# Gate stores, key reads and token-sum loads of an attention stage put in another order on the DMA queues

## The chip, the cores and the metric

The kernel runs on one core of one Trainium2 chip. The core's engines are TensorE (PE, with its weight loads shown apart as PEld), VectorE (DVE), ScalarE (ACT), GpSimd (POOL) and SyncE (SP), which only issues DMAs here; ACT issues some DMAs too. The metric is the device time of one execution in microseconds, the median of several runs. All matrix products run in float32 split in a high and a low part, so that one logical product is three passes (high by high, high by low, low by high).

## The reference

The input is 1024 tokens of width 1024, with 16 learned meta tokens put ahead (1040 rows). One block is computed:

```python
h = rms_norm(x)
q_a, k_a, v_a, q_b, k_b, v_b, gate_a, gate_b = split(h @ w_in)
y_a = differential_attention(q_a, k_a, v_a)    # 4 heads, two softmaxes each, full 1024 x 1040
y_b = windowed_gqa(q_b, k_b, v_b, sink)        # 8 heads, 128-token windows
m = sigmoid(gate_a) * (y_a @ w_ba) + sigmoid(gate_b) * (y_b @ w_bb)
h = x + m @ w_o
h = h + (silu(rms_norm(h) @ w_g) * (rms_norm(h) @ w_u)) @ w_d
out = rms_norm(h)[16:]
```

What matters for this change: the two gates are one product of all 1024 tokens with 2048 columns of `w_in`, and in differential attention each head has two score maps m = 0, 1 with the softmax of the one subtracted from that of the other.

## The kernel before

The stages follow each other: input norm and the projections of q, k and v with the windowed attention in between (to about 294 us of the span), then differential attention with the gate products as filler between its steps (294 to 626 us), then the branch products, the output product, and the feed-forward block (626 us to the end), which is nearly all matmuls.

*Projections.* `project_kva(h)` makes the keys of head h: `k_consume` (L656) stores each chunk of keys, high and low part, into a DRAM buffer `ka_d[h][m]` of 128 rows, 64 of the high part and 64 of the low part (L658). One DMA per map m and chunk; three chunks of 384, 384 and 272 columns.

*Loading a head.* `load_a(h)` (L922 on) issues, first for m = 1 and then for m = 0, the queries `aq` (L929) and the keys `ak` on SP. The keys are wanted twice on chip: as variant 0 with the high part in partitions 0 to 63 and the low part below (one DMA of 520 KB, L930), and as variant 1 with the two swapped (two DMAs of 260 KB, L932). `load_v(h)` (L938) brings the values `av` (L940 to L942). All loads of a head have one buffer each, so a head's loads wait for the last use by the head before.

*Scores.* `scores_a(h, t)` (L966) multiplies a tile of 128 queries with the keys, in three column chunks per map; the first chunk of the first map (m = 1, variant 0) is the first thing that needs `aq` and `ak`. DVE adds the distance bias (L969, L973), ACT takes the exponential (L977), DVE combines both maps (L983), `transpose_a` (L995 on PE, L998 on ACT, L999 on DVE) turns the tile and `values_a` (L1008) multiplies with `av`.

*Gates.* `gate_steps` (L868) computes the gate product with a Strassen-like scheme of seven products per column block k: in its first part the products named 1, 2 and 6 for all eight k (n = 0 to 23, in the order `first_g`), in the second the products 5, 7, 3, 4 of each k (n = 24 to 55). I write (k, p) for product p of block k; the order begins (0,1), (1,1), (0,2), (1,2), (2,1), (3,1), (2,2), (3,2), (4,1), (4,2). A product is 12 matmuls of 128x512, given out in four steps of three by `fill`. Two PSUM banks are shared by all. The products need sums of token halves and of weights: the weight operand `wopg` is made by POOL (L799 a cast, L800 a subtraction) from raw weights `wg` that SP loads (L760); the token sums were stored in DRAM as `t_d` earlier and are loaded over parts of the activations `hT_hi` and `hT_lo` by `turn_into(i)` (L820, two DMAs of 1 MB, for i = 1 eight of 256 KB), as soon as the products that use the old contents are out: i = 2 behind head 0's values, i = 0 after (7,1), i = 3 after (7,2), i = 1 after (4,6). i = 0 is first read by (0,5), i = 1 by (0,7), i = 3 by (0,4).

*Results of the gate products* leave PSUM by an ACT copy (L874, L881) or a DVE addition (L885, L899) into small tiles: tag `u` with 4 buffers for the parts kept, tag `g` with 3 buffers for finished ones. They are stored in `u_d` and `g_d`. For the first five blocks (k < 5) products 1 and 2 are stored by DMAs that ACT itself issues:

```python
nc.scalar.copy(p1, ps)
if k < 5:
    nc.scalar.dma_start(u_d[k], p1)
```

*Order.* A scheduler that simulates the engines orders the instructions on each engine, except inside `tc.manual_schedule(engines=...)`, where the program's own order holds for the engines named. One such stretch for PE and POOL opens ahead of the loop over the 32 (head, tile) pairs; at n = 5 (`BY_HAND`) it is closed, and one for PE alone is opened. For head 0 the loop starts with 24 steps of gate products (`G_FIRST`, six products), and only then come scores, five gate steps to a tile. `tc.issue_after(i)` only asks that an instruction stands behind i in its queue. The DMAs of the built program signal on eight semaphores used in rotation, whichever engine issues them; a DMA waits in its issuing engine's queue until the DMA eight before it has landed.

Of the kernel before, what the change touches and what calls it, by code (L numbers as in the profile page):

```python
# [19 lines left out]
P = 128  # L20
# [3 lines left out]
L = S + NM  # L24
# [24 lines left out]
WB_BUFS = 3  # L49
G_HEAD = 6  # L50
G_FIRST = 24
BY_HAND = 5

QK_BUFS = 3
W_BUFS = 2
# [20 lines left out]
def encoder_block(ctx: ExitStack, tc: tile.TileContext, x, meta, norm_mix, w_in, lq1, lk1, lq2, lk2,  # L76
# [7 lines left out]
    def f32(ap):  # L84
        return ap.bitcast(F32)
# [14 lines left out]
        return p.tile([P, 512], F32, tag=tag, name=name, bufs=bufs)  # L100

    qa_d = [dram.tile([2, P, S], F32, name=f"qa_d{h}") for h in range(AH)]
    ka_d = [dram.tile([2, P, L], F32, name=f"ka_d{h}") for h in range(AH)]
    va_d = [dram.tile([P, 2, 9, P], F32, name=f"va_d{h}") for h in range(AH)]
    g_d = [dram.tile([P, S], F32, name=f"g_d{i}") for i in range(16)]
    t_d = [dram.tile([P, 2, 4, 512], F32, name=f"t_d{i}") for i in range(4)]
# [548 lines left out]
    def project_kva(h):  # L655
        def k_consume(st, at, n):  # L656
            for m in range(2):
                nc.sync.dma_start(ka_d[h][m, :, at:at + n].rearrange("(a d) t -> d a t", a=2),  # L658
                                  st[64 * m:64 * m + 64, :, :n])

        def va_evac(pt, k0, nb, kp):
            vs = stage.tile([P, 2, 4, P], F32R, tag="qk", name="va_stage", bufs=QK_BUFS)
            hi, lo = vs[:kp, 0, :nb, :], vs[:kp, 1, :nb, :]
            nc.scalar.activation(hi, pt, AF.Copy)
            nc.vector.tensor_tensor(lo, pt, f32(hi), ALU.subtract)
            nc.sync.dma_start(va_d[h][:kp, :, k0:k0 + nb, :], f32(vs)[:kp, :, :nb, :])

        project_v(C_VA + h * P, f"va{h}", va_evac)
        project(C_KA + h * P, K_CHUNKS, f"ka{h}", evac_split(None, k_consume))
# [89 lines left out]
                    after.enter_context(tc.issue_after(keys_a[0].ins))  # L759
                raws_g.append(nc.sync.dma_start(w, w_in[:, col:col + P].rearrange("(c p) n -> p c n", p=P)))  # L760

    sums_g, keys_a, raws_g, values_in = {}, [], [], []

    def weights_g(n):
        k, p = order_g[n]
# [39 lines left out]
            n_made[0] += 1  # L805

    RIGHT_G = {1: (0, 0), 6: (0, 1), 2: (1, 0), 5: (0, 0), 7: (0, 1), 3: (1, 1), 4: (1, 0)}
    LAST_T = {(7, 1): (0,), (7, 2): (3,), (4, 6): (1,)}
    INTO_T = {2: (0, 1), 0: (0, 0), 1: (0, 1), 3: (1, 0)}

    def turn_into(i):

        d, t = INTO_T[i]
        for c in (range(4) if i == 1 else (slice(0, 4),)):
            for hl, h in enumerate((hT_hi, hT_lo)):
                with ExitStack() as after:
                    if i == 2:
                        after.enter_context(tc.issue_after(values_in[0].ins))
                    to = f32(h)[:, 4 * d:4 * d + 4, HALF[t]]
                    nc.sync.dma_start(to[:, c], t_d[i][:, hl, c])  # L820

    def gate_steps():
        banks, kept = {}, {}

        def stage_g(name):
            return gstage.tile([P, 512], F32, tag="g", name=name, bufs=G_BUFS)

        def kept_g(name):
            return gstage.tile([P, 512], F32, tag="u", name=name, bufs=4)

        def store(src, o, t, queue=nc.sync):
            queue.dma_start(g_d[o][:, HALF[t]], src)

        held_pp, last_pp = [None, None], [-1, -2]

        def take(n, k, p):
            i = min((i for i in range(2) if held_pp[i] is None), key=last_pp.__getitem__)
            held_pp[i], last_pp[i] = (k, p), n
            return bank(psum2, f"pp{i}", f"pg_{k}_{p}", 1)

        add = nc.vector.tensor_tensor
        for n, (k, p) in enumerate(order_g):
            ensure_g(n + 1)
            k_next = {(5, 1): 0, (6, 1): 1, (7, 1): 2, (7, 6): 3, (2, 6): 4, (3, 6): 0}.get((k, p), k + 1 if p == 7 and k < 7 else None)
# [12 lines left out]
            if p in (1, 2):  # L857
                banks[1, k] = banks.get((1, k), banks[1])
            ps = banks[1, k] if p in (1, 2) else banks[{3: 5, 4: 7}.get(p, p)]
            for i in range(2):  # L860
                if held_pp[i] == (k, {2: 1, 3: 5, 4: 7}.get(p, p)):
                    last_pp[i] = n
                    if p not in (1, 5, 7):
                        held_pp[i] = None
            d, t = RIGHT_G[p]
            for c in range(4):
                for i, (x, h) in enumerate(((0, hT_hi), (0, hT_lo), (1, hT_hi))):
                    nc.tensor.matmul(ps, op[:, x, c, :], h[:, 4 * d + c, HALF[t]],  # L868
                                     start=(p in (1, 6, 7) and c == 0 and i == 0),
                                     stop=(p in (2, 6, 3, 4) and c == 3 and i == 2), skip_group_check=True)  # L870
                if c == 3:
                    if p == 1:
                        p1 = kept_g(f"p1_{k}")
                        nc.scalar.copy(p1, ps)  # L874
                        if k < 5:
                            nc.scalar.dma_start(u_d[k], p1)
                        else:
                            kept[k] = p1
                    elif p == 2:
                        st = stage_g(f"g11_{k}")  # L880
                        nc.scalar.copy(st, ps)  # L881
                        store(st, 2 * k, 0, nc.scalar if k < 5 else nc.sync)
                    elif p == 6:
                        u = kept.pop(k)
                        add(u, ps, u, ALU.add)  # L885
                        nc.sync.dma_start(u_d[k], u)
                    elif p == 5:
                        kept["q"] = kept_g(f"q_{k}")
                        nc.scalar.copy(kept["q"], ps)
                    elif p == 7:  # L890
                        st = stage_g(f"g22_{k}")
                        add(st, ps, kept.pop("q"), ALU.add)
                        store(st, 2 * k + 1, 1)
                    else:
                        st = stage_g(f"g{p}_{k}")
                        if p == 3:
                            nc.scalar.copy(st, ps)
                        else:
                            add(st, ps, kept[k], ALU.add)  # L899
                        store(st, 2 * k + (p == 4), int(p == 3))  # L900
                    for i in LAST_T.get((k, p), ()):
                        turn_into(i)
                    if p == 4:
                        del kept[k]
                yield
            ensure_g(n + 4)
# [15 lines left out]
    def load_a(h):  # L922
        p = apool
        qs, ks = [None, None], [None, None]
        for m in (1, 0):
            q = qs[m] = p.tile([P, S], F32R, tag=f"q{m}", name=f"aq{h}_{m}")
            k = ks[m] = p.tile([P, 2, L], F32R, tag=f"k{m}", name=f"ak{h}_{m}")
            with tc.issue_after(raws_g[3].ins):
                nc.sync.dma_start(f32(q), qa_d[h][m])  # L929
            nc.sync.dma_start(f32(k)[:, 0, :], ka_d[h][m])  # L930
            for hl in range(2):
                last = nc.sync.dma_start(f32(k)[64 - 64 * hl:128 - 64 * hl, 1, :], ka_d[h][m, 64 * hl:64 * hl + 64, :])  # L932
        keys_a.append(last)
        v = p.tile([P, 2, 9, P], F32R, tag="v", name=f"av{h}")
        nc.gpsimd.memset(f32(v)[:, 0, 8, :], 0.0)
        return qs, ks, v

    def load_v(h, va):  # L938
        with tc.issue_after(keys_a[h].ins if h else raws_g[4].ins):
            nc.sync.dma_start(f32(va)[:, :, 0:8, :], va_d[h][:, :, 0:8, :])  # L940
            nc.sync.dma_start(f32(va)[:2 * NM, 0, 8, :], va_d[h][:2 * NM, 0, 8, :])
            values_in.append(nc.sync.dma_start(f32(va)[2 * NM:3 * NM, 0, 8, :], va_d[h][:NM, 1, 8, :]))  # L942
        if not h:
            turn_into(2)

    sum_a = {}

# [122 lines left out]

    for n in range(AH * NT + T_LAG):
        scoring, turning = iter(()), iter(())
        if n == BY_HAND:
            order_pe.__exit__(None, None, None)
            order_pe = tc.manual_schedule(engines={mybir.EngineType.PE})
            order_pe.__enter__()
        if n == 1:
            fill(2)
        if n < AH * NT:
            h, t = divmod(n, NT)  # L1080
            if t == 0:
                if not h:
                    ensure_g(2)
                ld = load_a(h)
                if h:
                    load_v(h, ld[2])
                fill(G_HEAD if h else G_FIRST)
                if not h:
                    load_v(h, ld[2])
            if t % 2 == 0:  # L1090
                at_ = apool.tile([P, 9, 2, 256], F32R, tag="at", name=f"at{h}_{t}", bufs=AT_BUFS)
            s = [None, None]
# [767 lines left out]
```

## Time and profile before

| | us |
|---|---|
| median of 3 runs | 1436.69 (1436.20 to 1436.83) |
| the profiled execution | 1435.76 |
| its span, first to last instruction | 1433.9 |
| TensorE busy in the span | 1404.5 (98%) |
| TensorE idle from 290 to 640 us | 19.0, of it one pause of 9.0 and one of 2.6 |

Times in the profile are microseconds from the start of the span. A timeline row gives start and duration, engine, line and operation, and, in brackets, how long the engine had stood idle and what ended that. ACTq and SPq are the issues of DMAs on those engines' queues; the time to landing counts from the issue. In a table of windows, each row is a stretch of the span with the busy time of each engine (and its instructions), the clock that TensorE was granted as a share of full speed, the DMA engines' busy share and the data rate.

### The profile page before, as it was taken

Reading aid. Unit: us, or ns where it says so; the run is one execution under the profiler, and the core shown is the slowest. Engines: PE = TensorE matmul, PEld = TensorE weight load, DVE = VectorE, ACT = ScalarE, POOL = GpSimd, SP = SyncE. Lnnn points to the kernel's source line nnn. Section 1 sums busy time; section 2 is a strip of 40 time slices with the busy share of each in tenths; the row PEclk is TensorE's granted clock in tenths of the full one; section 3 lists DMA queues with packets and bytes.
Section 4 is the critical chain, followed back from the end, with each engine's and each line's share of the span. In section 5 each row is a group of like instructions: output and inputs, shape, how many; then the busy total and the mean of one; then the engine's idle time right before and its main releaser. Section 6 shows DMA issues by size and latency. Waiting matters only on the chain.

```text
span 1433.9 us, 20696 instructions
## 1 busy us (share of the span) xinstructions
PE 1404.5 (98%) x7183; PEld 1205.7 (84%) x7183; DVE 911.6 (64%) x1584; ACT 672.5 (47%) x1284; POOL 634.6 (44%) x648
## 2 busy tenths in 40 slices
PE   9999999979999999999999999999999999999997
PEld 8998999968888888888888888888888888888886
DVE  6555666507778777755978966645544543787566
ACT  6355555414445554555346654333333333444454
POOL 4156865435677767232603044454544442000442
PEclk9999999989999999999999999999999999999999
DMA  8445564386696554197341624423332232954343
GB/s 235 95 127 161 147 199 141 101 273 195 200 327 208 166 163 148 38 317 235 116 154 75 206 88 144 150 97 109 106 107 96 96 109 99 359 183 144 121 130 141
DMA packets 193274, 226.15 MB, mean 158 GB/s; under 512 B 17336, under 2 KB 126336, under 8 KB 193168
## 3 DMA queue, kind: packets, MB, share of 16 engines
q1 hardware_dynamic: 189808, 219.36, 47.7%
q10 hardware_dynamic: 3360, 5.45, 1.2%
q8 instruction: 57, 0.93, 0.3%
q14 instruction: 49, 0.40, 0.1%
HBM read 152.48 MB, written 65.73 MB: 152 GB/s over the span
## 4 chain that ended last, share of the span: by engine, by line
PE 90%; DVE 4%; DMA 3%; ACT 1%; issue 1%; SPq 1%; POOL 0%; ACTq 0%; DVEq 0%; POOLq 0%
PE pg L1623 29%; PE pd L1727 14%; PE pg L868 7%; PE ppa L724 6%; PE po L1526 4%; PE aps L966 3%; PE pp_va L231 3%; PE pp_qb L231 3%; PE pp_qa L231 3%; PE pp_ka L231 3%; PE apy L1008 3%; DMA ak<-ka_d 2%; PE bps L398 2%; PE po L1534 2%; PE apt L995 1%; PE bpy L438 1%
## 5 line engine op out<-in xcount | busy, mean ns | idle before, releaser
L1623 PE MATMUL pg<-t,wop 128*128 128x512 f32 x1056 | 242.4, 389 | 0.0
L1623 PEld LDWEIGHTS pg<-t,wop 128*128 128x128 f32 x1056 | 198.3, 188 | 41.1
L121 POOL TENSOR_TENSOR wop<-wf,wop 128x512 fp32r<-128x512 f32 x114 | 150.7, 1323 | 164.1 <-ACT wop L120 152.7
L1727 PE MATMUL pd<-ob,oa 128*128 128x512 f32 x924 | 209.9, 389 | 0.0
L1727 PEld LDWEIGHTS pd<-ob,oa 128*128 128x128 f32 x924 | 173.3, 188 | 36.4 <-DVE ob L121 0.4
L1623 PE MATMUL pg<-b,wop 128*128 128x512 f32 x792 | 183.3, 389 | 0.0
L868 PE MATMUL pg<-hT_hi,wopg 128*128 128x512 f32 x448 | 171.9, 405 | 9.8 <-ACT g L881 9.0
L1623 PEld LDWEIGHTS pg<-b,wop 128*128 128x128 f32 x792 | 148.5, 188 | 30.7
L120 ACT ACTIVATE wop<-wf 128x512 fp32r<-128x512 f32 x128 | 80.7, 632 | 72.5 <-PE pg L1623 51.6
L121 POOL TENSOR_TENSOR oa<-ra,oa 128x512 fp32r<-128x512 f32 x27 | 34.9, 1294 | 168.9 <-ACT oa L120 167.5
L868 PEld LDWEIGHTS pg<-hT_hi,wopg 128*128 128x128 f32 x448 | 85.7, 191 | 22.6 <-issue 9.4
L977 ACT ACTIVATE as<-as,amn 128x1040 f32<-128x1040 f32 x64 | 74.5, 1165 | 59.0 <-DVE amn L973 59.0
L120 ACT ACTIVATE oa<-ra 128x512 fp32r<-128x512 f32 x77 | 48.7, 632 | 108.2 <-PE pd L1727 50.7
L966 PE MATMUL aps<-ak,aq 128*128 128x352 f32 (+1 forms) x384 | 87.7, 336 | 4.7 <-DMA ak<-ka_d 2.6
L969 DVE CUSTOM_DVE_ANT_0 as<-aps,dist,far_a 128x704 f32<-128x704 f32 x64 | 60.3, 942 | 48.9 <-POOL wopg L799 28.0
L868 PE MATMUL pg<-hT_lo,wopg 128*128 128x512 f32 x224 | 89.3, 399 | 0.0
L1400 DVE TENSOR_TENSOR s<-wf,wf 128x512 f32<-128x512 f32 x22 | 15.2, 693 | 110.7 <-DMA wf<-in_w_ff_up_dram 70.5
L966 PEld LDWEIGHTS aps<-ak,aq 128*128 128x128 f32 x384 | 65.1, 191 | 15.1 <-DVE amn L969 4.4
L400 DVE CUSTOM_DVE_ANT_0 bs<-bps,tbx,nsink 128x432 f32<-128x432 f32 (+1 forms) x64 | 38.5, 627 | 56.4 <-PE bps L398 34.9
L998 ACT ACTIVATE at<-apt 128x512 fp32r<-128x512 f32 (+1 forms) x96 | 45.3, 484 | 55.0 <-PE apt L995 55.0
L410 POOL TENSOR_SCALAR bs<-bs,bdn 128x432 f32<-128x432 f32 (+1 forms) x64 | 36.9, 596 | 76.7 <-DVE bdn L408 48.9
L1008 PEld LDWEIGHTS apy<-at,av 128*128 128x128 f32 x400 | 54.2, 190 | 4.1
(321 smaller groups left out, 3128.9 us busy)
## 6 DMA issues: line engine op xcount, KB each, us to landing
ra<-aop SPq DMA_DIRECT2D x77, 256.0 KB, 2.6
wf<-in_w_ff_gate_dram SPq DMA_DIRECT2D x25, 512.0 KB, 3.5
wf<-in_w_ff_up_dram SPq DMA_DIRECT2D x25, 512.0 KB, 3.6
aop<-as SPq DMA_DIRECT2D x44, 256.0 KB, 2.1
w_c<-in_w_in_dram SPq DMA_DIRECT2D x17, 512.0 KB, 4.9
aop<-c SPq DMA_DIRECT2D x33, 256.0 KB, 2.0
t_d<-tst SPq DMA_DIRECT2D x16, 512.0 KB, 4.1
wg_s<-in_w_in_dram SPq DMA_DIRECT2D x16, 512.0 KB, 6.2
```

The source lines that it names most:

```text
L120: high = nc.scalar.activation(hi, src, AF.Copy)
L121: lo_eng.tensor_tensor(lo, src, f32(hi), ALU.subtract)
L231: product = nc.tensor.matmul(ps[:, :n], a[:, c, :], b[:, c, at:at + n], start=(u == 0), stop=(u == 3 * DC - 1))
L724: nc.tensor.matmul(ps, w[:, a, j, :], src(j, b, tk), start=(j == 0 and n == 0), stop=(j == 3 and n == 2))
L868: nc.tensor.matmul(ps, op[:, x, c, :], h[:, 4 * d + c, HALF[t]], start=(p in (1, 6, 7) and c == 0 and i == 0), stop=(p in (2, 6, 3, 4) and ...
L966: nc.tensor.matmul(ps[:, :n], qs[m][:, t * P:(t + 1) * P], ks[m][:, vv, k0:k0 + n], start=(vv == 0), stop=(vv == 1))
L969: nc.vector.tensor_tensor_reduce(s[m][:, 0:2 * n].rearrange("p (a k) -> p a k", a=2), two[:, :, :n], dist[:, u0:u0 + 2 * n].rearrange("p ( ...
L977: nc.scalar.activation(s[m][:, 0:L], s[m][:, 0:L], AF.Exp, bias=mn[:, m, 1:2], scale=-1.0, accum_out=dn[:, 1:2] if m else first_sum)
L1008: nc.tensor.matmul(py[:, cols], v[:kp, a, k, :], at_[:kp, k, b, :], start=(k == 0 and j == 0), stop=(k == 8))
L1526: nc.tensor.matmul(sets_o[p][u], oa[:, a, u * P:(u + 1) * P], ob[:, b, :], start=(p in (1, 5) and j == 0 and k == 0), stop=(p in (2, 3) an ...
L1623: nc.tensor.matmul(ps, op[:, x, c, :], b[:, y, c, :], start=(p in (1, 5) and c == 0 and n == 0), stop=(p in (4, 2, 3) and c == 3 and n == ...
L1727: nc.tensor.matmul(ps[u], oa[:, a, u * P:(u + 1) * P], ob[:, b, :], start=(p in (1, 2, 5) and j == 0 and k == 0), stop=(p in (2, 3, 4) and ...
```

## The change

It has five parts.

1. Key storage: `ka_d` has 192 rows, and the high part of the keys is stored a second time in rows 128 to 191 (one more DMA per map and chunk: 24 in all).
2. Key reads: variant 1 is read by one DMA of 128 partitions from rows 64 to 191 instead of two of 64. A head's keys come in four DMAs, before in six.
3. Stores of gate results no longer go through ACT. `store` and the stores of `u_d` put them in a list, and `flush_stores` issues that list on SP, behind head 0's values.
4. Token sums: `turn_into(2)` comes after head 0's 24 gate steps, `turn_into(0)` after (7,6) and behind head 1's values, `turn_into(3)` together with `turn_into(1)` at (4,6) and behind `turn_into(0)`.
5. Order: for head 0 four weight operands are made ahead of the values' load, the values are loaded ahead of the 24 steps, and the stretch ordered by hand on PE and POOL ends right after those 24 steps (before, at n = 5), with a stretch for PE alone opened there.

```diff
-BY_HAND = 5
...
-    ka_d = [dram.tile([2, P, L], F32, name=f"ka_d{h}") for h in range(AH)]
+    ka_d = [dram.tile([2, 192, L], F32, name=f"ka_d{h}") for h in range(AH)]
...
             for m in range(2):
-                nc.sync.dma_start(ka_d[h][m, :, at:at + n].rearrange("(a d) t -> d a t", a=2),
+                nc.sync.dma_start(ka_d[h][m, 0:P, at:at + n].rearrange("(a d) t -> d a t", a=2),
                                   st[64 * m:64 * m + 64, :, :n])
+                nc.sync.dma_start(ka_d[h][m, P:192, at:at + n], st[64 * m:64 * m + 64, 0, :n])
...
-    LAST_T = {(7, 1): (0,), (7, 2): (3,), (4, 6): (1,)}
+    LAST_T = {(7, 6): (0,), (4, 6): (1, 3)}
...
                     if i == 2:
-                        after.enter_context(tc.issue_after(values_in[0].ins))
+                        after.enter_context(tc.issue_after(raws_g[5].ins))
+                    elif i == 0:
+                        after.enter_context(tc.issue_after(values_in[1].ins))
+                    elif i == 3:
+                        after.enter_context(tc.issue_after(turned_t[0].ins))
...
-        def store(src, o, t, queue=nc.sync):
-            queue.dma_start(g_d[o][:, HALF[t]], src)
+        held_stores = []
+
+        def store(src, o, t):
+            held_stores.append((g_d[o][:, HALF[t]], src))
+
+        def flush_stores():
+            if values_in:
+                with tc.issue_after(values_in[0].ins):
+                    while held_stores:
+                        nc.sync.dma_start(*held_stores.pop(0))
...
                         if k < 5:
-                            nc.scalar.dma_start(u_d[k], p1)
+                            held_stores.append((u_d[k], p1))
...
-                        store(st, 2 * k, 0, nc.scalar if k < 5 else nc.sync)
+                        store(st, 2 * k, 0)
...
-                        nc.sync.dma_start(u_d[k], u)
+                        held_stores.append((u_d[k], u))
...
+                    flush_stores()
...
-            nc.sync.dma_start(f32(k)[:, 0, :], ka_d[h][m])
-            for hl in range(2):
-                last = nc.sync.dma_start(f32(k)[64 - 64 * hl:128 - 64 * hl, 1, :], ka_d[h][m, 64 * hl:64 * hl + 64, :])
+            for v in range(2):
+                last = nc.sync.dma_start(f32(k)[:, v, :], ka_d[h][m, 64 * v:64 * v + P, :])
...
-        if not h:
-            turn_into(2)
...
-        if n == BY_HAND:
-            order_pe.__exit__(None, None, None)
-            order_pe = tc.manual_schedule(engines={mybir.EngineType.PE})
-            order_pe.__enter__()
...
                 ld = load_a(h)
-                if h:
-                    load_v(h, ld[2])
+                if not h:
+                    ensure_g(4)
+                load_v(h, ld[2])
                 fill(G_HEAD if h else G_FIRST)
                 if not h:
-                    load_v(h, ld[2])
+                    turn_into(2)
+                    order_pe.__exit__(None, None, None)
+                    order_pe = tc.manual_schedule(engines={mybir.EngineType.PE})
+                    order_pe.__enter__()
```

More of the change, by code (lines that the diff above doesn't have):

```diff
@@ L760, in load_g @@
                 raws_g.append(nc.sync.dma_start(w, w_in[:, col:col + P].rearrange("(c p) n -> p c n", p=P)))
-    sums_g, keys_a, raws_g, values_in = {}, [], [], []
+    sums_g, keys_a, raws_g, values_in, turned_t = {}, [], [], [], {}
     def weights_g(n):
@@ L817, in turn_into @@
                     if i == 2:
-                        after.enter_context(tc.issue_after(values_in[0].ins))
+                        after.enter_context(tc.issue_after(raws_g[5].ins))
[3 more added lines that the diff above has]
+                        after.enter_context(tc.issue_after(turned_t[0].ins))
                     to = f32(h)[:, 4 * d:4 * d + 4, HALF[t]]
-                    nc.sync.dma_start(to[:, c], t_d[i][:, hl, c])
+                    last = nc.sync.dma_start(to[:, c], t_d[i][:, hl, c])
+        turned_t[i] = last
     def gate_steps():
```

## The prediction

> **What bounds the kernel now.** I read the page first, then PE's waits, then the chain and the timelines around the waits found. The page says that PE bounds:
>
> ```profile
> span 1433.9 us, 20696 instructions
> ```
> ```profile
> PE 1404.5 (98%) x7183; PEld 1205.7 (84%) x7183; DVE 911.6 (64%) x1584; ACT 672.5 (47%) x1284; POOL 634.6 (44%) x648
> ```
>
> 29.4 us are idle, and the change removes no matmul, so it can gain only idle time and time at a lowered clock. PE's waits from 300 to 640 us (line, releaser, us in total, times, longest) show two single pauses:
>
> ```profile
> PE pg L868 <- ACT g L881: 9.0, 1, 9.0
> PE aps L966 <- DMA ak<-ka_d: 2.6, 1, 2.6
> ```
>
> The windows around both (stretch, PE, PEld, DVE, ACT, POOL busy, granted clock, DMA share, GB/s):
>
> ```profile
> 24.00:290.00 266.00, 266.00 (x1616) 245.78 (x1615) 157.40 (x380) 141.00 (x330) 146.26 (x155) 1.00 0.49 138
> 307.50:316.60 9.10, 0.09 (x2) 0.08 (x1) 0.00 (x0) 0.58 (x1) 2.96 (x4) 0.73 1.06 288
> 316.60:321.80 5.20, 5.20 (x12) 4.06 (x13) 0.00 (x0) 0.58 (x1) 1.89 (x2) 0.50 1.04 408
> 394.90:397.50 2.60, 0.00 (x1) 0.04 (x1) 0.00 (x0) 0.47 (x1) 2.40 (x2) 0.90 1.03 318
> 397.50:400.40 2.90, 2.90 (x9) 2.61 (x10) 1.56 (x3) 0.00 (x0) 1.92 (x3) 0.50 0.60 172
> ```
>
> After each pause PE has half its clock for a while. A gate matmul at full clock takes 0.227 us, from the first and the 60th of them in PE's timeline, (307.16 - 293.76)/59:
>
> ```profile
> 293.76 0.39 PE L868 MATMUL pg<-hT_hi,wopg 128*128 128x512 f32 x1
> ```
> ```profile
> 307.16 0.39 PE L868 MATMUL pg<-hT_hi,wopg 128*128 128x512 f32 x1
> 316.56 0.77 PE L868 MATMUL pg<-hT_hi,wopg 128*128 128x512 f32 x1 [9.01 <-ACT g L881]
> ```
>
> So 12 matmuls in 5.2 us lose 5.2 - 2.7 = 2.5, and 2.9 us at 0.50 lose 1.45. The first pause costs 9.0 + 2.5 = 11.5, the second 2.6 + 1.45 = 4.05. [...]
>
> ACT's timeline shows where the 9.0 come from:
>
> ```profile
> 302.14 0.59 ACT L881 COPY g<-pg 128x512 f32<-128x512 f32 x1 [2.13 <-PE pg L868]
> 315.38 0.33 ACTq L832 DMA_DIRECT2D g_d<-g  x1
> 315.82 0.58 ACT L881 COPY g<-pg 128x512 f32<-128x512 f32 x1 [13.09 <-DMA ak<-ka_d]
> ```
>
> The store of the copy made at 302.14 shares its semaphore with head 0's last key load and stands in ACT's queue until that landed, and the next copy, for which PE's bank waits, stands behind it. In the chain (start, us, what) those loads are:
>
> ```profile
> 298.70 2.07 SPq L929
> 300.87 6.90 DMA ak<-ka_d
> 307.78 7.52 DMA ak<-ka_d
> 316.56 5.46 PE pg L868 x12
> ```
> ```profile
> 388.53 8.83 DMA ak<-ka_d
> 397.50 1.22 PE aps L966 x3
> ```
>
> **The change, part by part.** *Stores off ACT: the first pause, -11.5.* Ten stores leave ACT's queue, so (3,1) no longer waits at 307.4.
>
> *What is late next on PE.* The hand-ordered stretch ends after the 24 gate steps, and in the changed kernel as built the scheduler has put head 0's first score matmul (variant 0 of m = 1) ahead of them: behind the second matmul of (1,2). That is 38 matmuls after 293.76, at this row:
>
> ```profile
> 302.40 0.61 PE L868 MATMUL pg<-hT_hi,wopg 128*128 128x512 f32 x2
> ```
>
> PE is in order there and stops until queries and keys have landed. Before, the first keys landed at 307.77 (chain: 300.87 + 6.90). Their time shifts twice. The keys' second store adds issues to an SP queue that is packed just ahead of the loads:
>
> ```profile
> 296.05 1.25 SPq L658 DMA_DIRECT2D ka_d<-qk_stage  x2
> 297.40 1.25 SPq L760 DMA_DIRECT2D wg_f<-in_w_in_dram  x2
> ```
>
> 0.62 us each; of those added I count three that find no idle time: +1.9. The other way, the two 256 KB stores that ACT issued here now come after the keys:
>
> ```profile
> 297.38 0.40 ACTq L876 DMA_DIRECT2D u_d<-p  x1
> ```
> ```profile
> 300.10 0.33 ACTq L876 DMA_DIRECT2D u_d<-p  x1
> ```
>
> From 307.78 to 315.30, 2.08 MB landed, 0.28 MB/us, so each is worth 0.9; the first had nearly landed before the keys started, so I count one and a half: -1.3. Landing at 308.4, bounds 305.9 (only the gain) and 309.7 (only the loss). PE stands 6.0 us (3.5 to 7.3), and between 1.45 and 2.5 for the half clock afterwards, I take 2.0: together 8.0 (5.0 to 9.8). The first pause thus shrinks by 3.5 (1.7 to 6.5).
>
> *The wait that takes its place on ACT.* Tag `g` has three buffers, so the fourth copy, of (3,2), needs the first store landed. That store now stands on SP behind head 0's values and both loads of token sums i = 2. In the rows of DMA issues (KB each, us to landing) the second of them, issued at 314.18, takes:
>
> ```profile
> hT_lo<-t_d SPq DMA_DIRECT2D x1, 1024.0 KB, 15.8
> ```
>
> It landed at 330.0, while ACT's queue moved four stores beside it that now come later, from that at 315.38 to
>
> ```profile
> 322.67 0.33 ACTq L876 DMA_DIRECT2D u_d<-p  x1
> ```
>
> (1.05 MB, 2.6 us at the window's 408 GB/s). 330.0 - 2.6, +0.6 for the later start, +0.7 for the store itself: 328.7. Then copy and exponential of tile 1:
>
> ```profile
> 332.04 1.16 ACT L977 ACTIVATE as<-as,amn 128x1040 f32<-128x1040 f32 x1
> 333.10 0.18 ACT L977 ACTIVATION_READ_ACCUMULATOR as<-as,amn 128x1 f32 x1
> 333.19 0.58 ACT L881 COPY g<-pg 128x512 f32<-128x512 f32 x1
> ```
>
> Before, the exponential came first; in the changed order the copy does. 328.7 + 0.6 is 329.3, I take 329.6 for issue times; against 332.04 that leaves 2.4 of the 3.5. Behind this exponential stand the copy of (4,1), for which (4,2) waits on PE, and tile 1's second exponential, for which its transposes wait; so 2.4 is what PE keeps. Bounds: if the token sums land no earlier (330.0 + 1.9 + 0.7 + 0.6 = 333.2) it is -1.2; if the store comes in time, up to 6.5. [...]
>
> *Keys of heads 1 to 3 in four DMAs: the second pause, -4.05.* Before, SP issued the last parts of head 1's keys behind a weight load, a wait of 2.69 for a semaphore and another store:
>
> ```profile
> 384.25 0.38 SPq L886 DMA_DIRECT2D u_d<-p  x1
> 384.72 0.39 SPq L760 DMA_DIRECT2D wg_m<-in_w_in_dram  x1
> 385.16 2.69 SPq L932 DMA_DIRECT2D ak<-ka_d  x1
> 387.94 0.54 SPq L1034 DMA_DIRECT2D ya_d<-yg  x1
> 388.53 0.45 SPq L932 DMA_DIRECT2D ak<-ka_d  x1
> ```
>
> In the changed order the last key load, now of 520 KB, stands right behind the first of these. At 384.6 + 8.83 + 0.93 for its 260 KB more it lands at 394.4, before PE ran dry at 394.9. It no longer stands behind that weight load, so I take the whole 4.05; the margin is 0.5, so the other end is 0.
>
> *Costs at nothing.* 24 more stores, 0.62 us of SP and at most 64 x 384 x 4 = 98 KB each: from 24 to 290 us PE is 266.00 busy and the DMAs at 0.49, which covers them; without cover they would cost up to 15. POOL's order in tiles 0 to 4 is the scheduler's: operands are made in another order, the tightest, for (2,2), is ready at the moment PE asks. I take 0, ends -1 and +1.
>
> *Token sums.* i = 0 is now issued after head 1's values, whose buffer came free at
>
> ```profile
> 412.80 0.21 POOL L935 MEMSET av<- 128x128 f32 x1 [0.95 <-PE apy L1008]
> ```
>
> 6.4 earlier that is 406.4; two us of issues and at worst 15.8 and the second MB's queue of 2.6 later, 427, it is in. Its reader (0,5) began at
>
> ```profile
> 435.69 0.48 PE L868 MATMUL pg<-hT_hi,wopg 128*128 128x512 f32 x1
> ```
>
> so 429.3: hidden, with 2 us to spare. i = 1 and i = 3 are read only by the products after it.
>
> **Sum.** -11.5 + 8.0 + 1.1 (ACT's wait) - 4.05 = -6.45. The profiled execution took 1435.76 (1433.9 in the span); it would take 1429.3. It ran 0.9 below the median of 1436.69, against which I predict 1430.3.
>
> **The rivals.** *The first pause only moves.* The keys land at 309.7 or the token sums at 333: the first part is worth 0, and head 1's keys alone give 1436.7 - 4.05 = 1432.6. For it: the DMAs are at 1.06 throughout, so any byte moved ahead of another delays it. Against it: the two ACT stores are out of the keys' way.
>
> *Keys early, store in time.* 6.5 + 4.05: 1426.1. It needs the keys at 305.9 and the store 3 us earlier than I have it.
>
> *Slower: (0,5) runs dry.* Values and i = 0 share one SP queue, which ran late before; the last load of head 1's values was issued at
>
> ```profile
> 421.17 0.55 SPq L942 DMA_DIRECT2D av<-va_d  x1
> ```
>
> If SP is no earlier now, i = 0 lands at 421.9 + 15.8 = 437.7, PE would stand 8.4 from 429.3 and lose 2.5 at half clock: 1430.3 + 10.9 = 1441.2. It decides against the change once the landing passes 438 on the new time scale. For it: the loads queue behind stores that wait for ACT and DVE. Against it: 4 MB of token sums that came first are now behind the values.
>
> *The change does not do what it says.* Head 1's last keys still miss 394.9: 1436.7 - 2.4 = 1434.3; with the first rival too, 1436.7.
>
> **How the numbers follow.** The forecast, 1428 to 1432, has 0.45; the first pause only moves, 0.20; keys early, 0.10; slower, 0.12; no effect on head 1, 0.13. About 0.2% (2.9 us: below 1433.8, above 1439.6) is what a measurement tells from no change. Faster is the first three without a fifth of the second, 0.71; slower 0.12; the same, 0.17. The range from 1426 to 1437 leaves out the slower case and half of the early one.
>
> **What would show it.** PE: no wait for the ACT copy at L881's place, but one of some 6 us for `ak` at 302.4 with half clock behind it; no wait for head 1's `ak`. ACT: a wait of 2 to 3 us ahead of the fourth copy of `g`, ended by a store or `t_d`. Wrong would be: PE standing at 302.4 for over 8 us, a wait of (0,5) for `t_d`, or POOL's operands ending PE's waits.

## The result, and the profile after

The changed kernel takes 1430.0 us (median of 6 runs, 1427.65 to 1430.64) against 1436.13 for the kernel before in the same comparison (6 runs, 1433.88 to 1436.83): ratio 0.9955, 95% interval 0.9943 to 0.9968. It is faster by 6.1 us; 1430.3 was predicted. The profiled execution took 1430.58 us, 1428.7 of them in the span. The page of the changed kernel begins:

```profile
span 1428.7 us, 20729 instructions
...
PE 1404.2 (98%) x7183; PEld 1205.1 (84%) x7183; DVE 917.9 (64%) x1584; ACT 672.7 (47%) x1284; POOL 636.9 (45%) x648
```

PE is busy for as long as before and idle for 5 us less. PE's waits of the changed kernel, 285 to 640 us (line, releaser, us in total, times, longest):

```profile
PE aps L977 <- DMA ak<-ka_d: 5.6, 1, 5.6
PE aps L977 <- DVE amn L980: 3.8, 12, 0.4
PE apt L1006 <- DVE as L994: 1.7, 1, 1.7
PE apt L1006 <- DVE adn L991: 1.1, 1, 1.1
PE apt L1006 <- DVE at L1010: 0.9, 2, 0.7
PE pg L881 <- ACT p L887: 0.8, 1, 0.8
PE ppa L724 <- DVE g L912: 0.8, 1, 0.8
```

The wait of 9.0 for ACT's copy and that of 2.6 for head 1's keys are gone; a new one of 5.6 stands at head 0's keys; the many small waits for DVE's `amn` are 12 instead of 7 (3.8 us, 2.0 before). In PE's timeline of the changed kernel (start, us; in brackets the idle time before it and what ended it) the first gate product, the new stop, the matmul of (4,2) and the first product after the gate stage:

```profile
294.99 0.39 PE L881 MATMUL pg<-hT_hi,wopg 128*128 128x512 f32 x1
...
309.38 0.63 PE L977 MATMUL aps<-ak,aq 128*128 128x352 f32 x1 [5.59 <-DMA ak<-ka_d]
...
334.11 0.50 PE L881 MATMUL pg<-hT_hi,wopg 128*128 128x512 f32 x1 [0.85 <-ACT p L887]
...
622.82 17.52 PE L724 MATMUL ppa<-yb,wbhb 128*128 128x512 f32 x76 [0.78 <-DVE g L912]
```

The last two of these in the kernel before:

```profile
336.54 0.50 PE L868 MATMUL pg<-hT_hi,wopg 128*128 128x512 f32 x1 [0.80 <-ACT p L874]
...
627.23 13.01 PE L724 MATMUL ppa<-yb,wbhb 128*128 128x512 f32 x56 [0.79 <-DVE g L899]
```

The gate stage, first gate product to first `ppa`, took 627.23 - 293.76 = 333.47 before and takes 622.82 - 294.99 = 327.83: 5.64 less. It began 1.23 later. In all the profiles of this study it begins between 292.91 and 294.99; the differences arise in the first 64 us, where nothing is changed, and then stay. So from here on times are counted from a profile's first gate product, and stages by their length.

Where in the stage the time came from is read off ACT's exponentials, two for each of the 32 tiles. The second one of tiles 11 and 12 in ACT's timeline before:

```profile
426.29 1.17 ACT L977 ACTIVATE as<-as,amn 128x1040 f32<-128x1040 f32 x1 [0.90 <-DVE amn L973]
...
434.97 1.17 ACT L977 ACTIVATE as<-as,amn 128x1040 f32<-128x1040 f32 x1
```

and after:

```profile
418.53 1.17 ACT L988 ACTIVATE as<-as,amn 128x1040 f32<-128x1040 f32 x1 [0.91 <-DVE amn L984]
...
429.08 1.17 ACT L988 ACTIVATE as<-as,amn 128x1040 f32<-128x1040 f32 x1 [1.20 <-DVE amn L984]
```

At tile 11 the changed kernel is ahead by (426.29 - 293.76) - (418.53 - 294.99) = 9.0, at tile 12 by 7.1. The same sum for every kernel of this study, as us later (+) or earlier (-) than the changed kernel's profile:

| kernel | tile 0 | tile 7 | tile 8 | tile 11 | tile 12 | tile 31 | stage, us |
|---|---|---|---|---|---|---|---|
| before | 3.7 | 4.7 | 8.8 | 9.0 | 7.1 | 5.6 | 333.47 |
| changed | 0 | 0 | 0 | 0 | 0 | 0 | 327.83 |
| e1 score matmul pinned | 1.2 | 1.1 | 1.1 | 1.1 | 1.1 | 1.6 | 329.45 |
| e2 hand order | -6.6 | -1.7 | -1.7 | -1.6 | -1.4 | -2.1 | 325.86 |
| e3 e1, sums i = 2 later | 0.1 | 1.4 | 1.4 | 1.4 | 1.4 | 1.5 | 329.40 |
| e4 e2, sums i = 2 later | -6.8 | -5.9 | -6.0 | -5.9 | -5.6 | -6.2 | 321.73 |
| e5 keys alone | 2.0 | 2.5 | 3.0 | 3.2 | 2.6 | 1.5 | 329.54 |
| e6 stores alone | -1.6 | 1.6 | 6.5 | 6.8 | 4.6 | 4.6 | 332.52 |
| e7 without keys | 2.6 | 3.9 | 5.0 | 5.1 | 5.1 | 6.5 | 334.96 |
| e8 without sums | -0.4 | -0.2 | -0.2 | -0.2 | -2.4 | -2.2 | 325.67 |
| e9 changed, again | 0.2 | 0.0 | 0.0 | 0.3 | 0.3 | -0.1 | 327.82 |
| e10 e8, again | 0.4 | 0.5 | 0.4 | 0.4 | -1.8 | -1.7 | 326.20 |
| e11 e8, POOL beside DVE | -0.2 | -0.7 | -0.7 | -0.7 | -2.9 | -2.7 | 325.42 |
| e12 e4 without sums | -6.4 | -5.9 | -5.9 | -4.9 | -3.3 | -4.0 | 323.93 |

The first row is the result in small: 3.7 to 4.7 us gained at head 0, 4.1 more between tiles 7 and 8 (head 1's keys), and 3.4 of it lost again between tile 11 and the end.

The windows around both old pauses in the changed kernel (stretch, PE, PEld, DVE, ACT, POOL busy, granted clock, DMA share, GB/s):

```profile
303.70:309.40 5.70, 0.11 (x2) 0.05 (x1) 0.00 (x0) 0.27 (x1) 4.24 (x5) 0.81 1.07 392
309.40:314.10 4.70, 4.70 (x12) 3.74 (x13) 0.00 (x0) 0.00 (x0) 0.00 (x0) 0.51 1.04 401
385.00:395.00 10.00, 10.00 (x61) 9.01 (x60) 4.53 (x12) 3.50 (x6) 6.44 (x8) 1.00 1.05 360
```

After the new stop 12 matmuls take 4.70 at clock 0.51 where they need 2.7 at 0.227: 5.6 + 2.0 = 7.6 in all. At head 1's keys there is no idle time and no lower clock; SP's timeline shows why, the last key load now stands right behind the store:

```profile
380.57 0.31 SPq L945 DMA_DIRECT2D ak<-ka_d  x1
380.99 0.37 SPq L845 DMA_DIRECT2D u_d<-p  x1
381.41 0.43 SPq L945 DMA_DIRECT2D ak<-ka_d  x1
```

And in ACT's timeline the wait for the store slot ahead of the fourth copy of `g`, and tile 1's exponential behind it:

```profile
328.50 0.59 ACT L894 COPY g<-pg 128x512 f32<-128x512 f32 x1 [2.51 <-DMA g_d<-g]
329.30 1.17 ACT L988 ACTIVATE as<-as,amn 128x1040 f32<-128x1040 f32 x1 [0.21 <-DVE amn L984]
```

### The profile page after: what moved, and what is told of

Same layout as the page of the kernel before. It is cut to its first block, busy times and chain, and to the rows that moved or that the text cites. A ratio compares the mean times of both kernels' runs of the same rounds, so it can differ in the third digit from the quotient of the medians.

```text
span 1428.7 us, 20729 instructions
## 1 busy us (share of the span) xinstructions
PE 1404.2 (98%) x7183; PEld 1205.1 (84%) x7183; DVE 917.9 (64%) x1584; ACT 672.7 (47%) x1284; POOL 636.9 (45%) x648
## 4 chain that ended last, share of the span: by engine, by line
PE 88%; DVE 6%; DMA 2%; ACT 2%; issue 1%; SPq 1%; POOL 0%; ACTq 0%; DVEq 0%; POOLq 0%
PE pg L1634 29%; PE pd L1738 15%; PE pg L881 8%; PE ppa L724 6%; PE po L1537 4%; PE pp_ka L230 3%; PE pp_va L230 3%; PE pp_qa L230 3%; PE aps L977 3%; PE apy L1019 2%; PE bps L397 2%; PE pp_qb L230 2%; PE po L1545 2%; DVE as L994 2%; DVE as L980 1%; PE bpy L437 1%
```

## The experiments

Theory A is the prediction's: at head 0 PE stops for the keys because the scheduler drew the score matmul forward, and if that stop goes, ACT's wait for the store slot takes its place. The rivals are given with each run. e1 to e4 shared one chip and one set of runs of the kernel before (median 1437.15, 11 runs), e5 to e8 another (1435.55, 24), e9 to e12 a third (1435.13, 9); between sets only the ratios are compared.

### Head 0: what is behind PE's stop

e1 pins head 0's first score matmul behind the last gate matmul of the 24 steps and leaves all else:

```diff
-                    nc.tensor.matmul(ps, op[:, x, c, :], h[:, 4 * d + c, HALF[t]],
+                    gate_mm[0] = nc.tensor.matmul(ps, op[:, x, c, :], h[:, 4 * d + c, HALF[t]],
...
+                    with ExitStack() as after:
+                        if (h, t, m, i, vv) == (0, 0, 1, 0, 0):
+                            after.enter_context(tc.issue_after(gate_mm[0].ins))
```

> The changed kernel with one edit: head 0's first score matmul must stand on PE behind the last matmul of the 24 gate steps. POOL stays with the scheduler. Theory A (the fourth copy of `g` takes over): the 5.6 us stop for head 0's keys and its half clock (2.3) go, but the first g_d store still lands at about 328.5 behind the token sums, so ACT stands about 10 us ahead of the fourth copy in place of 2.5, and tile 1's exponential begins at about 329 as before; PE then stands 5 to 8 us later, and the median is 1428 to 1430. Rival B (the store slot has slack, as the 2.5 us of ACT's wait that cost PE nothing suggest): nearly all 7.9 us come through, 1422 to 1424.

Measured: 1430.1 us (1428.34 to 1432.22), ratio 0.9953 [0.9937, 0.9968], that of the changed kernel. The time is that of theory A, at its upper end; the cause is not A's. In PE's timeline of e1:

```profile
318.38 0.80 PE L883 MATMUL pg<-hT_hi,wopg 128*128 128x512 f32 x1 [5.89 <-POOL wopg L800]
```

PE runs past the place of the keys and stops 5.9 us for an operand from POOL. POOL's timeline:

```profile
308.72 0.61 POOL L799 CAST wopg<-wg_f 128x512 fp32r<-128x512 f32 x1
316.50 0.61 POOL L799 CAST wopg<-wg_f 128x512 fp32r<-128x512 f32 x1 [7.16 <-DMA wg_f<-in_w_in_dram]
317.07 1.26 POOL L800 TENSOR_TENSOR wopg<-wg_f,wopg 128x512 fp32r<-128x512 f32 x1
```

An operand is made in two steps, a cast and a difference. The scheduler put the cast of another one between the two, and its weights landed only at 316.5; the difference, behind that cast in POOL's order, ran at 317.07. In the changed kernel the same order costs nothing, since PE is stopped by the keys at that time.

e2 restores the hand order of both engines up to tile 5, as the kernel before had it:

```diff
+BY_HAND = 5
...
+        if n == BY_HAND:
+            order_pe.__exit__(None, None, None)
+            order_pe = tc.manual_schedule(engines={mybir.EngineType.PE})
+            order_pe.__enter__()
...
                     turn_into(2)
-                    order_pe.__exit__(None, None, None)
-                    order_pe = tc.manual_schedule(engines={mybir.EngineType.PE})
-                    order_pe.__enter__()
```

> The changed kernel with PE and POOL in hand order up to tile 5, as the kernel before had it. PE's order at the gate is that of e1, POOL's the hand order. Theory A as for e1: the stop of PE goes and ACT's store slot takes its place. Theory C (POOL's free order costs about 2 us in many small waits for DVE between 400 and 626, of which the changed kernel has 6.4 us against 4.1): 1.5 to 2.5 us under e1. Rival D (those waits come from other things): within 0.7 of e1.

Measured: 1428.53 (1428.04 to 1429.04), ratio 0.9943 [0.9928, 0.9957], 1.6 under e1, though single runs of the two overlap. That is theory C's number, mainly for another reason than C's: what the free order of POOL costs first of all is one wait of 5.9 at head 0, which is gone. C's reason is not excluded beside it, for the small waits for `amn` fall too, from 3.6 us in e1 to 2.4. At tile 0 e2 is 6.6 ahead of the changed kernel, at tile 1 only 2.3, because now theory A's wait has come. PE's timeline of e2, then ACT's:

```profile
331.10 0.77 PE L882 MATMUL pg<-hT_hi,wopg 128*128 128x512 f32 x1 [4.55 <-ACT p L888]
```
```profile
328.35 0.58 ACT L895 COPY g<-pg 128x512 f32<-128x512 f32 x1 [4.33 <-DMA g_d<-g]
```

ACT waits for the slot until the same moment as in the changed kernel (328.4), but PE arrives earlier and pays 3.7 of it (4.55 against 0.85).

e3 and e4 take that cause away from e1 and e2: the token sums i = 2 are issued behind the first two g_d stores instead of ahead of them.

```diff
-                        nc.sync.dma_start(*held_stores.pop(0))
+                        stored.append(nc.sync.dma_start(*held_stores.pop(0)))
...
                     if i == 2:
-                        after.enter_context(tc.issue_after(raws_g[5].ins))
+                        after.enter_context(tc.issue_after(stored[3].ins))
```

> e1, and the two loads of token sums i = 2 stand on SP behind the first two g_d stores instead of ahead of them. Theory A: the first store then lands before 315, ACT doesn't stand ahead of the fourth copy, and the whole 5.6 + 2.3 us of the stop come through: 1421 to 1423, and e1 minus e3 is 5 to 8. Rival B: the slot never cost PE anything, e3 is within 1 of e1. Rival E: the token sums, 2 MB issued later, are late for (5,6): PE waits there for t_d and e3 is above e1.

> e2 and e3 together: hand order of PE and POOL to tile 5, and the token sums i = 2 behind the first two g_d stores. Theories A and C: 1419 to 1421. A without C: 1421 to 1423. Rival B: as e2.

Measured: e3 1429.66 (1428.88 to 1430.61), ratio 0.9952 [0.9937, 0.9967]; e4 1423.94 (1422.93 to 1425.05), ratio 0.9912 [0.9897, 0.9928]. In POOL's timeline of e4 the two steps of the operand stand together:

```profile
308.97 0.61 POOL L800 CAST wopg<-wg_f 128x512 fp32r<-128x512 f32 x1
309.67 1.29 POOL L801 TENSOR_TENSOR wopg<-wg_f,wopg 128x512 fp32r<-128x512 f32 x1
```

So three waits stand in line at head 0: the keys (PE's order), POOL's operand (POOL's order), the store slot (SP's order). Taking away the first gives nothing (e1, at the ratio of the changed kernel). Against e1, the first and the third together give 0.4 (e3), the first two 1.6 (e2), all three 6.2 us (e4). e3 alone looks as if the store slot cost nothing, which was rival B; against e2, e4 shows that it costs 4.6 once the two other waits are away. In neither does PE wait for token sums, so rival E falls.

### Which part of the change gives what

e5 is the kernel before with the keys' double store and two-part loads alone; e6 the kernel before with the stores' move alone, hand order kept; e7 the changed kernel without the keys' part; e8 the changed kernel without the token sums' part:

```diff
-    LAST_T = {(7, 6): (0,), (4, 6): (1, 3)}
+    LAST_T = {(7, 1): (0,), (7, 2): (3,), (4, 6): (1,)}
...
-                    elif i == 0:
-                        after.enter_context(tc.issue_after(values_in[1].ins))
-                    elif i == 3:
-                        after.enter_context(tc.issue_after(turned_t[0].ins))
```

For e7 (and e6) the loads and stores of keys are the old ones, for e5 the reverse of this:

```diff
-            for v in range(2):
-                last = nc.sync.dma_start(f32(k)[:, v, :], ka_d[h][m, 64 * v:64 * v + P, :])
+            nc.sync.dma_start(f32(k)[:, 0, :], ka_d[h][m])
+            for hl in range(2):
+                last = nc.sync.dma_start(f32(k)[64 - 64 * hl:128 - 64 * hl, 1, :], ka_d[h][m, 64 * hl:64 * hl + 64, :])
```

> The kernel before with the keys' double store and the two-part loads alone. My step (the second pause is the keys' form, 4.05 us): no wait of PE for head 1's `ak`; the first pause stays, 9.0 to 10.9 with up to three more issues ahead of the keys, since the store in ACT's queue still shares its semaphore with head 0's last key load: 2 to 4 us under before, ratio 0.997 to 0.9985. Rival (the second pause went because SP's other work was moved): PE's wait for head 1's `ak` is still there, and the ratio is 1.000 to 1.001.

> The kernel before with the stores' move alone (ACT's queue to SP, values ahead of the gate steps), PE's and POOL's hand order kept to tile 5 as before, keys and token sums as before. My sum's step: the first pause (11.5) goes and comes back in part as ACT's wait for the store slot, which in e2 cost 3.7 us of PE's time; head 1's pause of 4.05 stays: 3.5 to 6 us under before, ratio 0.996 to 0.9975, and 3 to 4.5 us over e2. Rival (head 1's keys come in time once the stores are gone, in their old form too): about the time of e2, ratio 0.994.

> The changed kernel without the keys' double store and two-part loads: keys stored once, loaded in three parts. My steps: head 1's wait for `ak` comes back (2.6 + 1.45), and head 0's keys land up to 1.9 earlier, so the stop of PE at the second matmul of (1,2) is shorter by up to 1.9: 2 to 4 us over the changed kernel, 1432 to 1434. Rival (the form of the keys does nothing, the order of SP does it): no wait for head 1's `ak`, 1428 to 1430.

> The changed kernel with the token sums of pass two where they were: i = 0 and i = 3 issued behind (7,1) and (7,2), ahead of head 1's values. My step (this part is worth nothing): within 1 us of the changed kernel, 1429 to 1431, with the profile's waits the same. Rival (the 4 MB of loads stand ahead of head 1's keys or values): a wait for `ak` or `av` appears between 380 and 420 and the time is 2 to 4 us higher.

Measured:

| kernel | median, us (range) | ratio to before [95%] |
|---|---|---|
| e5 keys alone | 1430.38 (1429.64 to 1432.18) | 0.9967 [0.9956, 0.9978] |
| e6 stores alone | 1433.22 (1430.46 to 1435.59) | 0.9982 [0.9970, 0.9995] |
| e7 without keys | 1434.55 (1431.40 to 1436.95) | 0.9994 [0.9985, 1.0004] |
| e8 without sums | 1427.33 (1426.41 to 1428.45) | 0.9945 [0.9932, 0.9957] |

The keys' part carries most of the change, and more than I gave it. At head 1 it does what was said. PE's waits of e5, then those of e6, which has the old loads, and the longest of these in e6's timeline:

```profile
PE aps L966 <- DMA ak<-ka_d: 0.2, 1, 0.2
```
```profile
PE aps L974 <- DMA ak<-ka_d: 8.0, 5, 3.4
```
```profile
395.09 0.72 PE L974 MATMUL aps<-ak,aq 128*128 128x352 f32 x3 [3.38 <-DMA ak<-ka_d]
```

Moving the stores alone leaves the wait there. The rival (SP's order did it) doesn't fall altogether, though: e7 has the old loads with the changed order of everything else on SP, and I had expected the whole pause back. PE's timeline of e7:

```profile
395.55 0.72 PE L977 MATMUL aps<-ak,aq 128*128 128x352 f32 x3 [0.93 <-DMA ak<-ka_d]
```

In the table above, the step from tile 7 to tile 8 against the changed kernel is 4.1 us before, 4.9 in e6, 1.1 in e7 and 0.5 in e5. So either the two-part loads or the changed order takes most of the pause away, and the two are not additive. In e7's order the weight load no longer stands ahead of the last keys; I have not tested that this is what helps.

The keys' part also gains at head 0, where I had booked it as a cost: e5 is 1.7 ahead of the kernel before at tile 0, and e7 2.6 behind the changed one. PE's waits of e5 show the first pause at 6.5, not 9.0 to 10.9:

```profile
PE pg L869 <- ACT g L882: 6.5, 1, 6.5
```

The windows show the reason. In e7, with the old loads, around PE's stop at head 0 (columns as above):

```profile
302.50:308.20 5.70, 0.17 (x2) 0.06 (x1) 0.00 (x0) 0.58 (x1) 4.04 (x5) 0.76 1.04 293
308.20:312.40 4.20, 1.93 (x5) 1.59 (x6) 0.00 (x0) 0.00 (x0) 0.00 (x0) 0.50 1.03 276
```

in e5, with the new ones:

```profile
309.70:316.30 6.60, 0.10 (x2) 0.05 (x1) 0.00 (x0) 0.59 (x1) 3.47 (x4) 0.82 1.06 388
```

With the DMA engines as busy (1.03 to 1.07), 276 to 293 GB/s are moved around the stop with the three-part loads (288 in the kernel before), 388 to 392 with the two-part ones. These stretches mix loads of both kinds. A narrower one in e7 runs from the landing of the first key load to that of the third, so that the two loads of 64 partitions land in it; beside it, a stretch of e5 in which only loads of 128 partitions land:

```profile
308.10:310.90 2.80, 0.63 (x1) 0.29 (x1) 0.00 (x0) 0.00 (x0) 0.00 (x0) 0.50 1.00 206
```
```profile
308.60:313.60 5.00, 1.18 (x6) 0.64 (x4) 0.00 (x0) 0.00 (x0) 4.52 (x6) 1.00 1.03 422
```

While loads of 64 partitions land, the DMA engines are as busy (1.00 against 1.03) and move half (206 against 422 GB/s); why they do, no run shows. In e7 PE therefore stops a second time, for 4.20 - 1.93 = 2.3 us of the second window, until the keys of variant 1 have landed, and e6's 8.0 us of waits for `ak` lie at head 0 for more than half. That fits both being slower than I expected.

### The token sums: a cost I had not counted

e8 came out below the changed kernel, with the gap opening between tiles 11 and 12. Two theories: F, the move itself costs it; G, it lay between chips or profiles. e9 is the changed kernel unaltered, e10 is e8 again, on one chip. e11 is e10 with one tensor-tensor of 128 x 384 more on POOL in 8 tiles, meant to run beside DVE's combination of the two score halves. e12 is e4 with e8's edit.

```diff
         nc.vector.scalar_tensor_tensor(s[0][:, 0:L], s[1][:, 0:L], dn[:, 0:1], s[0][:, 0:L], ALU.mult, ALU.add)
+        if (h, t) in BESIDE:
+            nc.gpsimd.tensor_tensor(beside, dist[:, 0:384], dn[:, 0:1].broadcast_to([P, 384]), ALU.add)
```

> The changed kernel once more, unaltered, on the same chip as the next three runs. Theory F (the token sums' move costs about 2 us between tile 12 and 15, as the exponentials' times show it): 1.5 to 3 us over the kernel without that part (e10). Rival G (the 2 us lay between two chips or two profiles): within 0.7 of it.

> e8 once more, on the same chip as e9. Theory F: 1427 to 1428.5, under e9 by 1.5 to 3. Rival G: as e9.

> e10 with one operation more on POOL in 8 of the 32 tiles (heads 1 and 2, tiles 4 to 7 of each): a tensor-tensor of 128 x 384 whose result nothing reads, which waits for the scalar that DVE's 128 x 1040 combination waits for, so that it runs beside that combination. Theory F (DVE's combination takes 1.3 us alone and up to 2.4 beside POOL, and PE's next score group waits for DVE): the combination's mean over these 8 rises by 0.5 to 1 us, PE's waits for `amn` grow, and the time is 2 to 6 us over e10. Rival G (DVE, 64% busy, has room for it): within 1 us of e10.

> e4 with the token sums of pass two back where they were before the change: hand order of PE and POOL to tile 5, token sums i = 2 behind the first two g_d stores, i = 0 and i = 3 ahead of head 1's values. Theory F: 1.5 to 3 us under e4's ratio of 0.9912, so 0.9892 to 0.9902, about 1421 to 1422.5. Rival G: ratio 0.991, about 1424.

| kernel | median, us (range) | ratio to before [95%] |
|---|---|---|
| e9 changed, again | 1429.16 (1428.44 to 1430.08) | 0.9953 [0.9940, 0.9965] |
| e10 without sums | 1428.10 (1426.98 to 1429.55) | 0.9944 [0.9932, 0.9957] |
| e11 POOL beside DVE | 1426.87 (1426.33 to 1427.66) | 0.9938 [0.9925, 0.9952] |
| e12 hand order, sums i = 2 later, i = 0 and 3 back | 1423.55 (1422.77 to 1424.90) | 0.9914 [0.9901, 0.9928] |

e9 and e10 differ by 1.1 us, between F's and G's bounds, and their runs overlap. The profiles repeat what e8's showed: level at tile 11, 2.1 apart at tile 12. At that place, DVE's timeline of e9 and, beside it, POOL's:

```profile
420.46 2.42 DVE L994 SCALAR_TENSOR_TENSOR as<-as,adn,as 128x1040 f32<-128x1040 f32 x1
```
```profile
419.92 0.61 POOL L799 CAST wopg<-wg_s 128x512 fp32r<-128x512 f32 x1
420.49 1.30 POOL L800 TENSOR_TENSOR wopg<-wg_s,wopg 128x512 fp32r<-128x512 f32 x1
```

and DVE's of e10, where POOL is idle from 419.25 to 419.96:

```profile
419.19 1.29 DVE L990 SCALAR_TENSOR_TENSOR as<-as,adn,as 128x1040 f32<-128x1040 f32 x1
```

In e9 DVE's combination, beside a POOL operation of 1.30, is 1.13 us longer (2.42 against 1.29), and PE then waits twice for `amn`. PE's timeline of e9:

```profile
424.60 0.91 PE L977 MATMUL aps<-ak,aq 128*128 128x352 f32 x4 [0.34 <-DVE amn L980]
...
433.49 0.91 PE L977 MATMUL aps<-ak,aq 128*128 128x352 f32 x4 [0.37 <-DVE amn L980]
```

and of e10, the same instruction as the second:

```profile
430.94 0.89 PE L973 MATMUL aps<-ak,aq 128*128 128x352 f32 x4
```

PE runs its matmuls in the same order in both kernels. Counted from the first gate product (294.40 and 293.00), e9's second one comes 1.15 us later than e10's, while the score group ahead of both waits (420.06 and 418.80) came 0.14 earlier. So on PE it is 1.3 us, less than ACT's exponentials show. But e11, which was to show the price of running beside POOL, didn't make what it was meant to make. Five of its eight added operations took 1.83 to 1.90 us, three 0.83. In the first of the two pairs below DVE's combination is the long one (1.97, POOL's operation 0.83), in the second it is POOL's operation (1.88, DVE's combination 1.30). POOL's timeline of e11, two of the eight, and DVE's at the same places:

```profile
425.81 0.83 POOL L994 TENSOR_TENSOR beside<-dist,adn 128x384 bf16<-128x384 f32 x1 [0.64 <-DVE adn L991]
...
434.90 1.88 POOL L994 TENSOR_TENSOR beside<-dist,adn 128x384 bf16<-128x384 f32 x1 [1.13 <-DVE adn L991]
```
```profile
425.76 1.97 DVE L992 SCALAR_TENSOR_TENSOR as<-as,adn,as 128x1040 f32<-128x1040 f32 x1
...
434.79 1.30 DVE L992 SCALAR_TENSOR_TENSOR as<-as,adn,as 128x1040 f32<-128x1040 f32 x1
```

Over all 32 tiles DVE's combination takes 1475 ns on the mean against 1497 in e10. With more work on POOL e11 is 1.2 us faster than e10 (their runs overlap). So the longer combination at tile 12 is seen, but that it is what the 1 to 2 us consist of is not shown, and what the move of the token sums costs stays open to that extent.

e12 shows what the move is good for. It is level with e4 (0.9914 and 0.9912), which is G's number. With i = 0 ahead of head 1's values, PE, which is 5 to 6 us earlier there than in the changed kernel, waits for those values. PE's waits of e12:

```profile
PE apy L1016 <- DMA av<-va_d: 2.0, 1, 2.0
```

In e8 and e10 PE comes later, and the values are in time without the move. e4 and e12 are the fastest versions of this study, about 6 us under the changed kernel by their ratios (0.9912 and 0.9914 against 0.9953 to 0.9955).

## Why the prediction was right

The total was right, 1430.3 against 1430.0, but partly by luck, because two errors cancelled: up to tile 11 the change gained 9.0, 2.5 more than the -6.45 of my sum, and later it lost 3.4 of which the sum had nothing. Of the 2.5, 1.1 is the store slot, which cost nothing; about 1.0 more arises between tiles 0 and 7 (3.7 and 4.7 in the table), and I have not traced it.

- *First pause, -11.5: right.* ACT's copy no longer waits behind the keys, and PE's wait of 9.0 is gone.
- *New stop for head 0's keys, +8.0: right in place, cause and size* (5.59 idle and 2.0 for the half clock, 7.6). At tile 0 the change is 3.7 ahead, where the sum has 11.5 - 8.0 = 3.5. What I took it for was incomplete: e1 shows POOL's operand right behind it. POOL's order, which I costed at "0, ends -1 and +1", is worth nothing only as long as PE stands there.
- *Head 0's keys, +1.9 - 1.3: about right for the landing that the sum used, incomplete for the part.* The first keys land at 309.25, 14.3 us into the stage, against 14.0 before and 14.6 in my sum. What I missed are the loads behind them. I priced the bytes at 0.28 MB/us, a rate taken from the three-part loads themselves, and didn't see that two-part loads raise it (388 to 392 GB/s around the stop against 276 to 293): with three-part loads PE would have stopped a second time (e7), and the wait for the last keys in the kernel before would have been shorter with two-part loads (e5). Net of the added issues, the keys' part gains 1.7 (e5) to 2.6 us (e7) at tile 0.
- *ACT's store slot, +1.1: the mis-sized term.* The wait is there, at 328.50 (328.7 predicted), 2.51 long, and the exponential at 329.30 (329.6). But counted from the first gate product it is 1.4 earlier than I had it. (4,2) begins 39.12 us into the stage against 42.78 before, 3.66 earlier, so PE keeps the whole 3.5 and the slot takes nothing from it. e2 shows that the mechanism is right: where PE arrives earlier, it pays 3.7. That the store lands behind the token sums ahead of it on SP was an estimate in the sum; in the changed kernel the second of those loads was issued at 317.08 and took 10.7, and the store, issued at 319.41, ended ACT's wait at 328.50.
- *Head 1's keys, -4.05: right in size, with more room than I gave it.* 4.1 between tiles 7 and 8. The last keys, issued at 381.41 and 7.3 us on the way, land 2.6 us ahead of the matmuls that read them (391.30), where I had a margin of 0.5. Two things help: e5 has most of the gain with the keys' part alone, e7 has most of it without, with the changed order on SP.
- *24 more stores, 0: right.* From 64 us to the gate stage all profiles of this study, with the doubled store and without, stay within 0.2 us of each other.
- *Token sums, hidden with 2 us to spare: right for the wait, wrong for the cost.* (0,5) doesn't wait for t_d. But the move costs about 1 us: 1.1 in the medians of e9 and e10, whose runs overlap, 1.3 on PE in their profiles, at the place where the loads were put.
- *What remains of the 3.4:* about 1.2 to 1.7 us between tile 11 and the end is lost against the kernel before also by e5, e6 and e8, none of which moves the token sums as the change does. I have no experiment for it.

Of the rivals, "the first pause only moves" was the nearest: at head 0 waits did move, from ACT to the keys, and would have moved on to POOL and to the store slot.

## What to carry to other kernels

When a wait is taken away, list everything that stands at the same place on the other engines, for the profile shows only the one that ends last. Here three orders (PE's, POOL's, SP's) each held a wait of 4 to 6 us, taking away one or two of them gave 0 to 1.6, and all together 6.2. Loads that fill 64 partitions at a time moved half the bytes in the same time as loads of all 128 (206 against 422 GB/s). And a rate read from a trace belongs to the shapes that were moved: here the 276 to 293 GB/s with the three-part loads didn't carry over to the two-part loads that the change brings (388 to 392).

## What the runs showed of the hardware

- 64-partition loads: 206 GB/s in a stretch in which two of them land (e7), against 422 with 128-partition loads alone (e5), and the DMA engines' busy share, 1.00 and 1.03, doesn't show the difference.
- DVE and POOL side by side: DVE's 128 x 1040 combination takes 1.30 and 1.28 with no POOL operation beside it (e11, at 578.01 and 594.43) and 2.42 beside a POOL operation of 1.30 (e9, at 420.46). With POOL's 128 x 384 beside it in e11, DVE's takes 1.97 and POOL's 0.83 in one pair (at 425.76), DVE's 1.30 and POOL's 1.88 in another (at 434.79). POOL's operation starts 0.05 and 0.11 us behind DVE's there; which of two came first can't be told from start times this close, and why one of the two takes longer was not shown.
- With nothing changed in it, the first 64 us differ by up to 2 us between profiles (the gate stage begins between 292.91 and 294.99), as much as some of the effects studied here. Stage lengths don't have that spread (327.83 and 327.82 for two profiles of the changed kernel, 325.67 and 326.20 for two without the sums' part).
